# Weight sums of a Strassen-type product: which of them are made by adding transfers and which by VectorE

## The chip, the cores and the metric

The kernel runs on one core of a Trainium2 chip. The metric is device time in microseconds (us), the median of several executions. The engines named here are PE (TensorE, matrix products), DVE (VectorE), ACT (ScalarE), POOL (GpSimd) and SP (SyncE). SP and POOL issue most of the DMA transfers, each into a queue of its own. A DMA issued by POOL can add what it carries to what lies at its destination; such a DMA is called an adding transfer here.

## The reference

One block of a streaming encoder on 256 frames of width 2048, all in float32: a half-step SwiGLU FFN, then two token mixers side by side (banded attention over chunks and retention) merged by sigmoid gates, then a second half-step FFN, and a final norm.

```python
def swiglu_ffn(x, w_gate, w_up, w_down):
    return (jax.nn.silu(x @ w_gate) * (x @ w_up)) @ w_down

x = x + 0.5 * swiglu_ffn(rmsnorm(x, norm_ffn1_g), ffn1_w_gate, ffn1_w_up, ffn1_w_down)
proj = rmsnorm(x, norm_mix_g) @ w_in                      # nine parts, 11264 columns
...                                                       # attention and retention
merged = sigmoid(gate_a) * (att @ w_out_att) + sigmoid(gate_r) * (ret @ w_out_ret)
x = x + merged @ w_out
x = x + 0.5 * swiglu_ffn(rmsnorm(x, norm_ffn2_g), ffn2_w_gate, ffn2_w_up, ffn2_w_down)
return rmsnorm(x, norm_final_g)
```

D_FF is 5632. Nearly all the time is matrix products of 256 rows with weights that are read once from DRAM.

## The kernel before

**Products.** A weight chunk has 2 x 128 rows and 512 columns (a tile 128 x 1024 in float32, 512 KB). Each product is made of three: the weight is split into a rounded part `hi` (an ACT copy, line 140) and the rest `lo` (a DVE subtraction, line 141), and `three` (lines 151, 152, 154) multiplies activation-hi by `hi`, activation-lo by `hi`, and last activation-hi by `lo`. So PE waits for `lo` only at line 154, after four or more products with `hi`.

**Steps.** The work of PE is a list of steps, one per weight chunk. A standard step (class `Gemm`: the down products, some projections) makes 12 products, a step of the class `Strassen` makes 6. `run` goes through the list. Ahead of a step it calls `prep_upto`, which writes the split of the steps up to four ahead into the streams of ACT and DVE (there are four split buffers), and then the work that `later(n, ...)` has put off by n steps.

**Groups.** A `Strassen` object computes two blocks of 512 columns at once, here w1 and w2 (for an FFN: up and gate), with seven products of half size in place of eight. With `a0`, `a1` for the upper and lower rows of w1 and `b0`, `b1` for those of w2, each of the four chunks jc = 0..3 passes through these sums:

- `loads`: tile `k` gets a0 and tile `x` gets b0, by DMAs on POOL's queue (line 540).
- first sum: x = b0 + a0. Either DVE makes it (`first`, line 529) or an adding transfer from tile to tile on POOL's queue (`add_on`, line 545).
- second sum: x = x + b1 (line 597, DVE). b1 is in the tile `raw` that SP's queue fetched for a product of its own.
- `third`: k = x - a0 on DVE (line 583), and then x = x + a1 by an adding transfer from DRAM (line 584).

A group has seven runs of four steps, named by phase and kind: phase 0 has `r` (a0) and `s` (the first sum), phase 1 `r` (b1) and `s` (the second sum), phase 2 `r` (a1) and `s` (k), phase 3 `s` (x after the third). The tile names say it: `loz15401s` is the `lo` part of group z154, phase 0, jc 1, kind s; a name `lo<-raw,hi` without a z belongs to a standard step. `weave` puts standard steps between the steps of the groups.

There are 26 groups: ten in each FFN (the names z10 to z334 and z706 to z1030) and six in the mixer's projections (z390 to z565). `ADDED`, `MIX_ADDED` and `FIRST_ADDED` say for which jc the first sum is an adding transfer: none in the first group of the mixer and of the second FFN; jc 2 and 3 in the very first group, z10; jc 0 in the mixer's other five and in the second group of each FFN (z46, z742); jc 0 and 1 in the other sixteen groups of the FFNs.

**Order.** Engines work through their streams in order. POOL's stream is nearly only DMA issues. SP fetches `raw` tiles into five buffers, as soon as one is free.

Of the kernel before, what the change touches and what calls it, by code (L numbers as in the profile page):

```python
# [11 lines left out]
ALU = mybir.AluOpType  # L12
# [29 lines left out]
RET_WAIT = (14, 6)  # L42
RET_PUT = ((3, 5), (2, 2))
HELD = 6
MIX_ADDED = (0,)
FIRST_ADDED = (2, 3)
MIX_AHEAD = 12
FIRST_WAIT = 4
LAST_SUM = 24
ROTATED = {("q", 0): (6, 7), ("k", 0): (5, 6), ("q", 1): (4, 5), ("k", 1): (3, 4)}  # L50
HEAD_AT = (3, 6, 10, 13, 17, 20, 24, 27)

MIX_SHARE = (0.5,) * 4 + (1.0,) * 4 + (0.0,) * 4 + (0.2,) * 4
SHARE = (0.75,) * 4 + (1.0,) * 4 + (0.0,) * 4 + (0.2,) * 4
ADDED = (0, 1)
ADD_WAIT = 6
PLAIN = 10
PASSES = ((10,),) + tuple((b,) for b in range(10))
# [28 lines left out]
def block_kernel(ctx: ExitStack, tc: tile.TileContext, x, g1, w1g, w1u, w1d, gm, w_in, rel, woa, wor, wo,  # L87
                 g2, w2g, w2u, w2d, gf, cos, sin, decay, ident, out):
    nc = tc.nc
# [30 lines left out]
    def later(n, fn):  # L120
        due.setdefault(state["step"] + n, []).append(fn)

    def weights_tile(name):
        return wpool.tile([P, KC, NB], F32, tag="raw", bufs=RAW_BUFS, name=name)

    def chunk(w, r0, c0):
        return w[r0 : r0 + KC * P, c0 : c0 + NB].rearrange("(k p) n -> p k n", p=P)

    def fetch(t, w, r0, c0, parts=(slice(0, KC),)):
        for p in parts:  # L130
            nc.sync.dma_start(t[:, p, :], chunk(w, r0, c0)[:, p, :])

    def split_tiles(name):
        return [
            wpool.tile([P, KC, NB], F32R, tag=tag, bufs=SPLIT_BUFS, name=f"{tag}{name}") for tag in ("hi", "lo")
        ]

    def split(raw, name):
        hi, lo = split_tiles(name)
        nc.scalar.copy(hi, raw)  # L140
        nc.vector.tensor_sub(lo, raw, hi.bitcast(F32))  # L141
        return hi, lo
# [3 lines left out]
    def three(products, read_between=False):  # L146


        more = {"skip_group_check": True} if read_between else {}
        for acc, (ahi, alo), (whi, _), first, _ in products:  # L150
            nc.tensor.matmul(acc, ahi, whi, start=first, stop=False, **more)  # L151
            nc.tensor.matmul(acc, alo, whi, start=False, stop=False, **more)  # L152
        for acc, (ahi, _), (_, wlo), _, last in products:
            nc.tensor.matmul(acc, ahi, wlo, start=False, stop=last, **more)  # L154
# [216 lines left out]
    class Operand:  # L371


        def __init__(self, name, n):
            self.hi, self.lo, self.name = [None] * n, [None] * n, name
# [18 lines left out]
    class Norm:  # L394
# [40 lines left out]
        def put(self, b, halves=(0, 1), between=None):  # L435
# [28 lines left out]
            elif 1 in halves and b % 2 == 1:  # L464
                for i, key in enumerate(self.SUMS):
                    wait = LAST_SUM if key == "s7" and self.name != "n1" and b == D // NB - 1 else 1 + 3 * i
                    later(wait, lambda key=key: self.add_up(b // 2, key))
# [39 lines left out]
    class Strassen:  # L507
# [3 lines left out]

        def __init__(self, norm, w1, col1, w2, col2, evict, added=()):
            self.added, self.summed = added, set()
            self.add_wait, self.early = ADD_WAIT, False
            self.norm, self.w, self.col, self.evict = norm, (w1, w2), (col1, col2), evict
            self.x, self.kept, self.acc, self.wide = {}, {}, {}, {}
            self.name = f"z{len(steps)}"
# [17 lines left out]
        def loads(self):  # L535
# [11 lines left out]
            def second(jc):  # L547
# [3 lines left out]
                elif self.early:  # L551
                    later(FIRST_WAIT, lambda: self.first_once(jc))

# [16 lines left out]
        def step(self, phase, jc, of_sum):  # L570
            made = {}
            name = f"{self.name}{phase}{jc}{'rs'[of_sum]}"
            n = HALF_K // KC

            def load():
                made["raw"] = weights_tile(f"raw{name}")
                i = 2 - phase
                fetch(made["raw"], self.w[i], self.rows(1, jc), self.col[i])

            def third():  # L580

                x, k = self.x[jc], self.kept[jc]
                nc.vector.tensor_sub(k, x, k)
                nc.gpsimd.dma_start(x, chunk(self.w[0], self.rows(1, jc), self.col[0]), accum_op=ALU.add)

            def prep():
                x = self.x[jc]
                if not of_sum:
                    if phase == 0:
                        made["w"] = split(self.kept[jc], name)  # L590
                        if jc not in self.added and not self.early:
                            self.first_once(jc)
                        return
                    raw = made.pop("raw")
                    made["w"] = split(raw, name)
                    if phase == 1:
                        nc.vector.tensor_add(x, x, raw)
                elif phase == 2:
                    made["w"] = split(self.kept.pop(jc), name)
                elif phase == 3:  # L600
                    made["w"] = split(self.x.pop(jc), name)
                else:
                    if phase == 0:
                        self.first_once(jc)
                    made["w"] = split(x, name)
                    if phase == 1:
                        third()

            bank, form, fresh, closing = {
# [4 lines left out]
            }[phase, of_sum]  # L614

            def products():
                hi, lo = made["w"]
                if fresh and jc == 0:
                    self.bank(bank)
                three([  # L620
                    (
                        self.acc[bank], self.norm.form(form, KC * jc + i), (hi[:, i, :], lo[:, i, :]),
                        fresh and jc == 0 and i == 0, closing and jc == n - 1 and i == KC - 1,
                    )
                    for i in range(KC)
                ], True)
                if jc == n - 1:
                    self.end(phase, of_sum)

            loaded = not of_sum and phase in (1, 2)  # L630
            frees = ["raw"] if loaded else ["kept"] if of_sum and phase > 1 else []
            return Step(self, 0, load if loaded else None, prep, frees, products)

        def end(self, phase, of_sum):
# [103 lines left out]
    def ffn(name, norm, wg, wu, wd, after, start=None):  # L738
# [41 lines left out]
        def paired(b):  # L780
# [10 lines left out]

            return Strassen(norm, wu, b * NB, wg, b * NB, evict, ADDED)

# [282 lines left out]
    def gates(col1, col2, func, dsts):  # L1076
# [9 lines left out]

        return Strassen(nm, w_in0, col1, w_in0, col2, evict, MIX_ADDED)

# [6 lines left out]
    def queries():  # L1095
# [9 lines left out]

        return Strassen(nm, w_in0, QA, w_in0, QA + NB, evict, MIX_ADDED)

# [90 lines left out]
    def at(step, fn):  # L1198
        due.setdefault(step, []).append(fn)
# [60 lines left out]
    for step, fn in merges:  # L1260
        at(step - 8, fn)
# [64 lines left out]
```

## Time and profile before

| | before |
|---|---|
| median of 3 runs | 2037.09 us (2036.96 to 2037.99) |
| profiled execution | 2037.64 us |
| its span, first to last instruction | 2035.9 us |
| PE busy | 2023.9 us (99%) |
| DVE busy | 1786.5 us (88%) |
| ACT busy | 1504.3 us (74%) |
| POOL busy | 342.9 us (17%) |
| moved by DMA | 504.77 MB |
| of it on POOL's queue (q0) | 196.80 MB |
| of it on SP's queue (q1) | 297.31 MB |
| granted clock of PE | 0.999 |

The time of an execution is some 2 us more than its span. A row of the timeline has the start and the length of an instruction in us, engine, line, operation and tiles, its form, and in square brackets how long the engine had stood idle and who ended that. Instructions on DVE overlap a little: one that follows on another starts before the other's recorded end. A row of windows ends with the granted clock, the share of time in which the 16 DMA engines were at work (records overlap, so it can pass 1), and GB/s.

### The profile page before, as it was taken

The page shows a single profiled execution, that of the slowest core. Times are in us where ns is not written, and L with a number is a line of the kernel's source. Part 1 is how long each engine was busy: PE and PEld are TensorE (multiplying, and loading weights), DVE is VectorE, ACT ScalarE, POOL GpSimd, SP SyncE. Part 2 cuts the span into 40 slices and gives each one's busy share as a digit, 9 for nine tenths or more (in the row PEclk, how much of TensorE's full clock was granted, in tenths as well). Part 3 has the DMA queues.
Part 4 walks back from the last instruction along what each step waited for, and adds up shares of the span by engine and source line. Part 5 has one row for each costly group of instructions (what it writes and reads, how often), then busy time and mean ns, then how long its engine had stood idle before and what let it go on. Part 6 is the DMA issues. An engine that isn't in the chain of part 4 may idle for free.

```text
span 2035.9 us, 26220 instructions
## 1 busy us (share of the span) xinstructions
PE 2023.9 (99%) x9170; PEld 1678.8 (82%) x9170; DVE 1786.5 (88%) x1823; ACT 1504.3 (74%) x1886; POOL 342.9 (17%) x399
## 2 busy tenths in 40 slices
PE   9999999999999999999999999999999999999998
PEld 7788888888888888888888888888888888888886
DVE  7999999999998898999987677569999999999996
ACT  7788888878888777777765434557788888888885
POOL 1221122212112021111120000011112221122200
PEclk9999999999999999999999999999999999999999
DMA  9888899988878689899897645576889988889974
GB/s 311 255 249 258 255 269 281 262 240 250 260 235 237 218 232 303 273 283 286 256 320 236 209 156 185 186 247 188 263 268 276 274 243 237 258 269 270 285 199 135
DMA packets 226436, 504.77 MB, mean 248 GB/s; under 512 B 15776, under 2 KB 16480, under 8 KB 226304
## 3 DMA queue, kind: packets, MB, share of 16 engines
q1 hardware_dynamic: 154560, 297.31, 43.1%
q0 software_dynamic: 67536, 196.80, 37.4%
q10 hardware_dynamic: 4208, 8.99, 1.2%
q8 instruction: 72, 1.18, 0.2%
q14 instruction: 60, 0.49, 0.1%
HBM read 471.04 MB, written 10.50 MB: 237 GB/s over the span
## 4 chain that ended last, share of the span: by engine, by line
PE 98%; DVE 0%; DMA 0%; ACT 0%; issue 0%; POOL 0%; DVEq 0%; POOLq 0%; ACTq 0%; SPq 0%
PE acc L152 15%; PE acc L151 15%; PE acc L154 15%; DMA raw<-in_ffn_w_gate_dram 0%; PE z298a L152 0%; PE z530a L151 0%; PE z425a L151 0%; PE z850a L152 0%; PE z154a L152 0%; PE z1030a L152 0%; PE z994a L152 0%; PE z565a L151 0%; PE z742a L152 0%; PE z334a L152 0%; PE z118a L152 0%; PE z886a L152 0%
## 5 line engine op out<-in xcount | busy, mean ns | idle before, releaser
L141 DVE TENSOR_TENSOR lo<-raw,hi 128x1024 fp32r<-128x1024 f32 x351 | 427.7, 1221 | 118.7 <-ACT hi L140 113.8
L140 ACT CAST hi<-raw 128x1024 fp32r<-128x1024 f32 x351 | 368.0, 1050 | 178.0 <-PE acc L152 134.0
L808 ACT ACTIVATE xall<-acc 128x512 f32<-128x512 f32 x160 | 94.6, 591 | 13.4 <-PE acc L154 9.3
L805 ACT ACTIVATE acc<-xall 128x512 f32<-128x512 f32 x160 | 95.9, 600 | 2.5
L151 PE MATMUL acc<-hi,mgh 128*128 128x512 f32 x128 | 50.2, 392 | 0.0
L152 PE MATMUL acc<-hi,mgl 128*128 128x512 f32 x128 | 49.8, 389 | 0.0
L154 PE MATMUL acc<-lo,mgh 128*128 128x512 f32 x128 | 35.5, 390 | 0.0
L151 PE MATMUL acc<-hi,nma01h 128*128 128x512 f32 x80 | 32.0, 400 | 0.0
L151 PE MATMUL acc<-hi,nma00h 128*128 128x512 f32 x80 | 31.9, 398 | 0.0
L152 PE MATMUL acc<-hi,nma01l 128*128 128x512 f32 x80 | 31.2, 390 | 0.0
L152 PE MATMUL acc<-hi,nma00l 128*128 128x512 f32 x80 | 31.2, 390 | 0.0
L151 PE MATMUL acc<-hi,nma11h 128*128 128x512 f32 x80 | 31.2, 390 | 0.0
L151 PE MATMUL acc<-hi,nma10h 128*128 128x512 f32 x80 | 31.2, 390 | 0.0
L152 PE MATMUL acc<-hi,nma11l 128*128 128x512 f32 x80 | 31.2, 390 | 0.0
L152 PE MATMUL acc<-hi,nma10l 128*128 128x512 f32 x80 | 31.2, 390 | 0.0
L154 PEld LDWEIGHTS acc<-lo,mgh 128*128 128x128 f32 x128 | 24.0, 188 | 5.0
L151 PEld LDWEIGHTS acc<-hi,mgh 128*128 128x128 f32 x128 | 24.0, 188 | 4.9
L152 PEld LDWEIGHTS acc<-hi,mgl 128*128 128x128 f32 x128 | 24.1, 188 | 4.8
L151 PE MATMUL acc<-hi,atth 128*128 128x512 f32 x64 | 25.7, 402 | 0.0
L151 PE MATMUL acc<-hi,reth 128*128 128x512 f32 x64 | 25.3, 395 | 0.0
L359 POOL TENSOR_TENSOR n2rstd<-v,mhalf 128x2 f32<-128x2 f32 x1 | 0.7, 695 | 144.6 <-DVE v L358 144.6
L152 PE MATMUL acc<-hi,attl 128*128 128x512 f32 x64 | 25.0, 390 | 0.0
(6885 smaller groups left out, 7279.9 us busy)
## 6 DMA issues: line engine op xcount, KB each, us to landing
raw<-in_ffn_w_down_dram SPq DMA_DIRECT2D x176, 512.0 KB, 7.1
raw<-in_w_in_dram SPq DMA_DIRECT2D x80, 512.0 KB, 5.7
raw<-in_w_out_dram SPq DMA_DIRECT2D x32, 512.0 KB, 3.7
raw<-in_ffn_w_up_dram SPq DMA_DIRECT2D x16, 512.0 KB, 4.9
raw<-in_w_out_att_dram SPq DMA_DIRECT2D x16, 512.0 KB, 3.9
raw<-in_w_out_ret_dram SPq DMA_DIRECT2D x16, 512.0 KB, 3.7
raw<-in_ffn_w_gate_dram SPq DMA_DIRECT2D x15, 512.0 KB, 4.9
z390x<-in_w_in_dram POOLq DMA_DIRECT2D x8, 512.0 KB, 8.8
```

The source lines that it names most:

```text
L140: nc.scalar.copy(hi, raw)
L141: nc.vector.tensor_sub(lo, raw, hi.bitcast(F32))
L151: nc.tensor.matmul(acc, ahi, whi, start=first, stop=False, **more)
L152: nc.tensor.matmul(acc, alo, whi, start=False, stop=False, **more)
L154: nc.tensor.matmul(acc, ahi, wlo, start=False, stop=last, **more)
L359: nc.gpsimd.tensor_tensor(dst, v, mhalf[:, :width], op=ALU.pow)
L805: nc.scalar.activation(acc, xs[t][:, cols], AF.Copy, scale=2.0)
L808: nc.scalar.activation(xs[t][:, cols], acc, AF.Copy, scale=0.5)
```

## The change

The first sums are now all made by DVE but for the two of z10 (jc 2 and 3). The second sums are no longer made by DVE: an adding transfer reads b1 from DRAM again and adds it to `x`. It is put off by two steps behind the split of the step phase 0 `s` of the same jc. The tile `raw` with b1 is still fetched by SP for its own product.

```diff
-MIX_ADDED = (0,)
+MIX_ADDED = ()
 FIRST_ADDED = (2, 3)
...
+SECOND_WAIT = 2
...
-ADDED = (0, 1)
+ADDED = ()
...
-            self.add_wait, self.early = ADD_WAIT, False
+            self.add_wait, self.early, self.adds_second = ADD_WAIT, False, True
...
+            def second():
+                nc.gpsimd.dma_start(self.x[jc], chunk(self.w[1], self.rows(1, jc), self.col[1]), accum_op=ALU.add)
...
                     made["w"] = split(raw, name)
-                    if phase == 1:
+                    if phase == 1 and not self.adds_second:
                         nc.vector.tensor_add(x, x, raw)
...
                     if phase == 0:
                         self.first_once(jc)
                     made["w"] = split(x, name)
+                    if phase == 0 and self.adds_second:
+                        later(SECOND_WAIT, second)
                     if phase == 1:
                         third()
```

The streams of PE, ACT and SP keep their order. In the streams of DVE and POOL rows appear and go. Below, a number behind a tile's name is its buffer, and lines 141, 529, 540, 545, 583 and 584 of before are lines 142, 530, 541, 546, 587 and 588 of the changed kernel.

DVE at the beginning of phase 0 of group z154, one of the sixteen groups, before:

```order
L141 TENSOR_TENSOR loz15400r<-z154k_2035,hiz15400r 128x1024
L141 TENSOR_TENSOR loz15401r<-z154k_2443,hiz15401r 128x1024
L141 TENSOR_TENSOR lo_2618<-raw_2417,hi_2617 128x1024
L141 TENSOR_TENSOR loz15400s<-z154x_2059,hiz15400s 128x1024
L788 SCALAR_TENSOR_TENSOR z118c_2557<-z118a,n1rstd,z118c_2557 128x512
L141 TENSOR_TENSOR loz15402r<-z154k_2499,hiz15402r 128x1024
L529 TENSOR_TENSOR z154x_2511<-z154x_2511,z154k_2499 128x1024
```

and the same place now:

```order
L142 TENSOR_TENSOR loz15400r<-z154k_2033,hiz15400r 128x1024
L530 TENSOR_TENSOR z154x_2057<-z154x_2057,z154k_2033 128x1024
L142 TENSOR_TENSOR loz15401r<-z154k_2442,hiz15401r 128x1024
L530 TENSOR_TENSOR z154x_2473<-z154x_2473,z154k_2442 128x1024
L142 TENSOR_TENSOR lo_2618<-raw_2416,hi_2617 128x1024
L142 TENSOR_TENSOR loz15400s<-z154x_2057,hiz15400s 128x1024
L794 SCALAR_TENSOR_TENSOR z118c_2555<-z118a,n1rstd,z118c_2555 128x512
L142 TENSOR_TENSOR loz15402r<-z154k_2498,hiz15402r 128x1024
L530 TENSOR_TENSOR z154x_2510<-z154x_2510,z154k_2498 128x1024
```

The first sums of jc 0 and 1 now stand in front of the `lo` of the standard step (`lo_2618`).

DVE at the beginning of phase 1 of the same group, before:

```order
L141 TENSOR_TENSOR loz15410r<-rawz15410r,hiz15410r 128x1024
L597 TENSOR_TENSOR z154x_2059<-z154x_2059,rawz15410r 128x1024
L141 TENSOR_TENSOR loz15411r<-rawz15411r,hiz15411r 128x1024
L597 TENSOR_TENSOR z154x_2474<-z154x_2474,rawz15411r 128x1024
L141 TENSOR_TENSOR lo_2784<-raw_2621,hi_2783 128x1024
L141 TENSOR_TENSOR loz15410s<-z154x_2059,hiz15410s 128x1024
```

and now:

```order
L142 TENSOR_TENSOR loz15410r<-rawz15410r,hiz15410r 128x1024
L142 TENSOR_TENSOR loz15411r<-rawz15411r,hiz15411r 128x1024
L142 TENSOR_TENSOR lo_2785<-raw_2621,hi_2784 128x1024
L142 TENSOR_TENSOR loz15410s<-z154x_2057,hiz15410s 128x1024
L587 TENSOR_TENSOR z154k_2033<-z154x_2057,z154k_2033 128x1024
```

The second sums are gone from DVE; what follows them has moved up.

POOL from the last loads of z154 to the third sums, before:

```order
L540 DMA z154x_2547<-in_ffn_w_gate_dram 128x2x512
L545 DMA z154x_2474<-z154k_2443 128x1024
L540 DMA z190k_2563<-in_ffn_w_up_dram 128x2x512
L540 DMA z190x_2587<-in_ffn_w_gate_dram 128x2x512
L545 DMA z190x_2587<-z190k_2563 128x1024
L584 DMA z154x_2059<-in_ffn_w_up_dram 128x2x512
```

and now:

```order
L541 DMA z154x_2546<-in_ffn_w_gate_dram 128x2x512
L541 DMA z190k_2561<-in_ffn_w_up_dram 128x2x512
L541 DMA z190x_2585<-in_ffn_w_gate_dram 128x2x512
L582 DMA z154x_2057<-in_ffn_w_gate_dram 128x2x512
L582 DMA z154x_2473<-in_ffn_w_gate_dram 128x2x512
L582 DMA z154x_2510<-in_ffn_w_gate_dram 128x2x512
L582 DMA z154x_2546<-in_ffn_w_gate_dram 128x2x512
L588 DMA z154x_2057<-in_ffn_w_up_dram 128x2x512
```

The two adding transfers from tile to tile are gone, and four from DRAM (line 582) stand between the next group's first loads and the third sums.

## Prediction

> **What bounds the kernel now.** I first read the page's busy times, then windows, then the timeline of one group.
>
> ```profile
> PE 2023.9 (99%) x9170; PEld 1678.8 (82%) x9170; DVE 1786.5 (88%) x1823; ACT 1504.3 (74%) x1886; POOL 342.9 (17%) x399
> 500.00:550.00 50.00, 50.00 (x227) 41.48 (x226) 45.70 (x44) 41.61 (x52) 10.13 (x12) 1.00 0.89 263
> 0.00:50.00 50.00, 47.30 (x208) 37.34 (x209) 36.66 (x46) 38.53 (x69) 9.31 (x17) 1.00 0.94 317
> 50.00:100.00 50.00, 49.49 (x220) 39.91 (x219) 49.97 (x53) 39.47 (x48) 14.25 (x16) 1.00 0.87 246
> 2000.00:2050.00 50.00, 27.13 (x131) 22.74 (x130) 21.28 (x32) 17.19 (x33) 1.12 (x2) 0.92 0.22 73
> ```
>
> In a window the columns are PE, PE's weight loads, DVE, ACT and POOL, then clock, DMA share and GB/s. From about 90 us to the tail PE is busy in every microsecond at full clock. All its idle time is 2035.9 - 2023.9 = 12.0 us: 2.7 us in the first 50 us, 0.5 us in the next 50, and 35.9 - 27.1 = 8.8 us behind 2000 us, in the tail. So VectorE, at 88%, does not set the end, and what the change takes off it is worth nothing by itself. The question is whether anything now makes PE wait.
>
> How near PE is to waiting is read from the gap between the end of a `lo` on DVE and PE's first product with it. Group z154, one of the sixteen FFN groups with two adding transfers before:
>
> ```profile
> 281.41 1.22 DVE L141 TENSOR_TENSOR loz11833s<-z118x,hiz11833s 128x1024 fp32r<-128x1024 f32 x1 [1.87 <-ACT hiz11833s L140]
> 282.55 0.68 DVE L659 TENSOR_TENSOR z118c<-z118c,z118s 128x512 f32<-128x512 f32 x1
> 283.15 1.22 DVE L141 TENSOR_TENSOR loz15400r<-z154k,hiz15400r 128x1024 fp32r<-128x1024 f32 x1
> 284.29 1.22 DVE L141 TENSOR_TENSOR loz15401r<-z154k,hiz15401r 128x1024 fp32r<-128x1024 f32 x1
> 285.42 1.22 DVE L141 TENSOR_TENSOR lo<-raw,hi 128x1024 fp32r<-128x1024 f32 x1
> 286.56 1.22 DVE L141 TENSOR_TENSOR loz15400s<-z154x,hiz15400s 128x1024 fp32r<-128x1024 f32 x1
> 286.87 0.62 PE L154 MATMUL z154a<-loz15401r,n1a00h 128*128 128x512 f32 x2
> 288.23 0.61 PE L154 MATMUL acc<-lo,f1a2h 128*128 128x512 f32 x2
> 290.95 0.62 PE L154 MATMUL z154c<-loz15400s,n1s5h 128*128 128x512 f32 x2
> ```
>
> DVE waits for ACT at 281.41 and then runs without a pause, one 128x1024 operation every 1.135 us. PE takes `loz15401r` 286.87 - 285.51 = 1.36 us after its end, the standard `lo` 288.23 - 286.64 = 1.59 us, `loz15400s` 290.95 - 287.78 = 3.17 us. These are the margins that the change eats.
>
> **The change part by part.** *First sums.* The engine's existing first sums show the price:
>
> ```profile
> L529 DVE TENSOR_TENSOR z154x<-z154x,z154k x2: 1217/1217/1217, 289.5 to 292.9; 128x1024 f32<-128x1024 f32 x2
> L545 POOL DMA_DIRECT2D z82x<-z82k x2: 927/927/927, 111.9 to 155.6; - x2
> L545 POOL DMA_DIRECT2D z1030x<-z1030k x2: 924/927/930, 1875.1 to 1919.7; - x2
> 1502.79 1.22 DVE L141 TENSOR_TENSOR lo<-raw,hi 128x1024 fp32r<-128x1024 f32 x1
> 1505.60 0.61 PE L154 MATMUL acc<-lo,f2a0h 128*128 128x512 f32 x2
> ```
>
> By the stream of the changed kernel, both added sums of such a group stand ahead of the standard `lo`, one of them ahead of `loz15401r`. Beginning at 283.15 as before (DVE still starts on ACT's `hiz11833s`, whose stream is the same), DVE runs `loz15400r` 283.15, sum 284.29, `loz15401r` 285.42, sum 286.56, `lo` 287.69 to 288.91. `loz15401r` keeps 1.36 - 1.14 = 0.22 us. The standard `lo` is late: PE wants it at 288.23. How long after the end of a late `lo` PE goes on is seen in z10, where PE did wait a little:
>
> ```profile
> 78.10 1.22 DVE L141 TENSOR_TENSOR loz1020r<-rawz1020r,hiz1020r 128x1024 fp32r<-128x1024 f32 x1
> 79.37 0.73 PE L154 MATMUL z10b<-loz1020r,n1a01h 128*128 128x512 f32 x2
> ```
>
> The `lo` ends at 79.32, PE starts at 79.37: 0.05 us. So PE starts at 288.96 instead of 288.23: **0.73 us lost**. PE has no idle time later in the group to make it good, and ACT and DVE reach the next group's start paced by PE, so each group loses it anew. Behind it all later margins are shortened by 2 x 1.135 = 2.27 us and lengthened by the 0.73 us that PE is later: `loz15400s` keeps 1.6 us. ACT's `hiz15400s` must now wait for the first sum's end at 285.51, some 0.8 us later than it began, but it was not DVE's limit there.
>
> The pattern is the same in z82 to z334 and in z778 to z1030 (the rows at 1502.79 and 1505.60: 1505.60 - 1504.01 = 1.59 us again, lost 0.73 us): 16 x 0.73 = **+11.7 us**. Bounds: 0 if the chain began earlier than I think; and, if the 0.22 us of `loz15401r` were not there either, 16 x 2.27 = 36 us as the whole of the added DVE time. I take 11.7, since both ends of the subtraction are rows.
>
> In z46 and z742 only one sum joins, and DVE stood idle for 0.90 us where it lands; in the five mixer groups also one, with a nearest margin of 886.89 - 884.87 = 2.02 us against 1.135 us of delay. Both cost nothing; if that slack were gone, 7 x 1.1 = 8 us.
>
> ```profile
> 102.81 1.23 DVE L141 TENSOR_TENSOR lo<-raw,hi 128x1024 fp32r<-128x1024 f32 x1 [0.90 <-ACT hi L140]
> 883.65 1.22 DVE L141 TENSOR_TENSOR loz49500s<-z495x,hiz49500s 128x1024 fp32r<-128x1024 f32 x1
> 886.89 0.62 PE L154 MATMUL z495c<-loz49500s,nms5h 128*128 128x512 f32 x2
> ```
>
> *Second sums off DVE.* 104 of 1.135 us go, 39 come: 65 x 1.135 = 74 us less DVE work, in phase 1, where PE does not wait now. Only z10 gains: PE's 0.5 us of idle time between 50 and 100 us lies behind its phase 1 backlog, as at 79.37. **-0.5 us** (bounds 0 and -0.5).
>
> *Second sums on the DMA.* The nearest rows are the third sums, the same kind and size from DRAM:
>
> ```profile
> L584 POOL DMA_DIRECT2D z154x<-in_ffn_w_up_dram x4: 1194/1194/1211, 309.8 to 323.4; - x4
> DMA to landing us min/median/max: 5.7/6.2/13.3
> 293.88 0.92 POOL L545 DMA_DIRECT2D z190x<-z190k  x1 [13.90 <-DMA z190x<-in_ffn_w_gate_dram]
> 309.83 1.21 POOL L584 DMA_DIRECT2D z154x<-in_ffn_w_up_dram  x1 [15.02 <-ACT xall L808]
> 304.28 1.06 ACT L140 CAST hiz15410s<-z154x 128x1024 fp32r<-128x1024 f32 x1 [0.59 <-PE acc L152]
> 317.34 1.06 ACT L140 CAST hiz15413s<-z154x 128x1024 fp32r<-128x1024 f32 x1 [1.13 <-DVE z154x L597]
> 297.50 1.22 DVE L141 TENSOR_TENSOR loz15403s<-z154x,hiz15403s 128x1024 fp32r<-128x1024 f32 x1
> ```
>
> POOL has nothing else to do between 294.8 and 309.8, so it issues each second sum when the `lo` of its first sum is done: jc 0 near 290 (287.8 + 2.27), jc 3 near 301 (298.7 + 2.27). On POOL only the third sums queue behind these waits, and they come later anyway. Landing after some 6 us means 296 and 307, wanted by ACT at 304.3 and 317.3: 8 to 10 us to spare, and even the longest landing, 13.3 us, reaches jc 3 only at 314. Cost 0.
>
> What remains is the bandwidth.
>
> ```profile
> 254.00:290.00 36.00, 36.00 (x160) 29.84 (x159) 33.27 (x32) 28.39 (x34) 10.40 (x12) 1.00 1.04 318
> 290.00:314.00 24.00, 24.00 (x111) 19.96 (x111) 22.60 (x22) 20.76 (x27) 2.13 (x2) 1.00 0.66 175
> 254.00:314.70 60.70, 60.70 (x273) 50.38 (x272) 56.58 (x53) 49.14 (x60) 12.53 (x14) 1.00 0.89 260
> 854.00:911.00 57.00, 57.00 (x253) 47.20 (x252) 53.96 (x49) 41.76 (x45) 11.49 (x14) 1.00 0.93 287
> q0 software_dynamic: 545, 1.07, 72.2%
> q1 hardware_dynamic: 564, 1.09, 38.1%
> q0 software_dynamic: 544, 1.05, 53.8%
> q0 software_dynamic: 148, 0.54, 20.8%
> ```
>
> The last four rows are queues, with packets, MB and share of the 16 engines. From 862 to 870 us POOL's queue q0 carries third sums: 0.722 x 8 us for 1.07 MB, so 2.8 us of all 16 engines for 0.52 MB; SP's q1 stands below it. From 310 to 322 us it is 0.538 x 12 us for 1.05 MB, 3.2 us for 0.52 MB. From 292 to 309 us q0 has one adding transfer between tiles: 0.208 x 17 = 3.5 us. An FFN group gains 4 x 2.8 and loses 2 x 3.5: +4.2 us on 54 of 60.7, so 0.95 to 0.96, against 1.04 in the stretch where the engines are full. They land where the share is 0.66, between the full stretches. A mixer group gains 11.2 - 3.5 = 7.7 us on 53 of 57: 1.06, just what a full stretch shows. I take 0 for the FFNs and 0 for the mixer, with 10 us as the mixer's upper bound: 60.7 us of load less 1.04 x 57 = 59.3 is 1.4 us per group, and at 3.2 us per second sum 3.0 us. Six groups give 8 to 18 us before buffers take any of it; I put it at 10.
>
> The Trainium skill, "DMA: Bandwidth & Descriptors", section "Anatomy of one DMA", gives the data part of a transfer as bytes over 436 GB/s, 1.2 us for 0.52 MB. The rows above have 2.8 us for an adding one, so here the measurement decides; by the page the mixer group would stay at 0.95 and the sum the same.
>
> **Sum.** In the profiled execution: 2037.64 + 11.7 - 0.5 = 2048.8 us. The median of the runs is 0.55 us under that execution, so I predict **2048.3 us**.
>
> **Rivals.**
> - *Hidden: no measurable change, 2036.6 us* (2037.1 - 0.5). DVE would have to start its chain at least 0.7 us earlier against PE. For it: ACT loses a wait for the old adding transfer at jc 1:
>
> ```profile
> 289.36 1.05 ACT L140 CAST hiz15401s<-z154x 128x1024 fp32r<-128x1024 f32 x1 [2.59 <-DMA z154x<-z154k]
> ```
>
>   Against: that wait of 2.59 us lies behind the late `lo`, and the chain starts on ACT's `hi` for the group before.
> - *DMA full: slower still, about 2058 us.* In the mixer `raw` tiles or the next group's `k` and `x` land late, as the shares allow: 2048.3 + 10. It decides from the point where the mixer's load passes what a full stretch carries. In its favour, 1.06 by shares; against it, shares are swollen by contention, and each mixer group has a stretch of low share. The same skill page, section "Issuing engines are not separate DMA queues", says that transfers from all queues share the 16 engines; the trace agrees (from 862 to 870 us the shares of the two queues sum to 1.10).
> - *Faster, between 2025 and 2033 us.* VectorE at 88% is the hidden bound, and 74 us less work shortens stalls that PE's row does not show, the matmuls being modelled. The most it can give is all of PE's idle time: 2037.1 - 12.0 = 2025 us. But the margins above are positive everywhere outside z10, so 0.5 us is all that I can find.
> - *The second sums are still on DVE*: no, the stream shows them gone.
>
> **How the numbers follow.** Late `lo`: 0.66. DMA full on top of it: 0.17. Hidden: 0.12. Faster: 0.05. Within the likeliest case I expect 2044 to 2053 us (0.45 to 1.0 us lost per group). To hold the time 8 times in 10 the range reaches into the DMA case and towards the hidden one: 2040 to 2061 us. A measurement of this kernel tells about 0.2% (4 us) from no change. Slower by more than that takes the first two cases less a part that comes out under 4 us: 0.80. Within: 0.16. Faster: 0.04.
>
> **What would show it.** In the changed profile: PE idle time of some 0.7 us once in each of the sixteen groups, before a product of line 154 with a standard `lo`, put down to DVE, with two sums ahead of it; groups 61.4 us apart instead of 60.7; no PE idle time in phase 1 and in z46 and z742; DVE busy near 1786 - 65 x 1.2 = 1708 us; second sums landed well before their `hi` on ACT; about 54.5 - 20.4 = 34 MB more moved. It is wrong if PE shows no idle time there, or if it waits for ACT behind `raw`, `k` or `x` landing late, above all between 750 and 1050 us.

## The result and the profile after

| | before | after |
|---|---|---|
| median of 4 runs each, on one chip | 2037.39 us | **2051.14 us** (2050.79 to 2052.51) |
| ratio, with its 95% interval | | 1.0068 (1.0056 to 1.0081) |
| profiled execution | 2037.64 us | 2052.51 us |
| its span | 2035.9 us | 2050.7 us |

The change costs 13.7 us. The changed kernel's page, engines first, then what was moved and POOL's queue (packets, MB, share of the 16 engines):

```profile
PE 2029.5 (99%) x9170; PEld 1677.1 (82%) x9170; DVE 1727.2 (84%) x1758; ACT 1503.2 (73%) x1886; POOL 432.3 (21%) x464
DMA packets 249111, 538.87 MB, mean 263 GB/s; under 512 B 16817, under 2 KB 17521, under 8 KB 248977
q0 software_dynamic: 90208, 230.88, 46.4%
```

DVE has 65 instructions fewer and 59 us less busy time, 34.1 MB more were moved, and the span is 14.8 us longer. PE has as many products as before. Its busy time grew by 5.6 us; the rest is 9.2 us more idle time. Windows of the changed kernel (PE, weight loads, DVE, ACT, POOL, clock, DMA share, GB/s) say where:

```profile
50.00:100.00 50.00, 48.88 (x216) 39.13 (x215) 45.06 (x48) 38.38 (x47) 15.66 (x17) 1.00 1.03 286
500.00:550.00 50.00, 49.45 (x222) 40.69 (x221) 45.82 (x43) 40.09 (x50) 13.02 (x15) 1.00 0.98 287
850.00:900.00 50.00, 50.00 (x222) 41.39 (x221) 44.36 (x40) 34.97 (x38) 13.07 (x14) 1.00 1.06 333
900.00:950.00 50.00, 50.00 (x223) 41.39 (x222) 44.02 (x40) 37.56 (x41) 13.01 (x14) 1.00 1.07 315
```

An FFN window that was full before now has 0.55 us of idle time (500 to 550 us); z10's window has lost another 0.6 us (it had 49.49); the mixer's windows are full, though their DMA share is 1.06 to 1.07.

The beginning of group z154 in the changed kernel's timeline (start, length; the last row of PE has the idle time and its releaser in brackets):

```profile
285.33 1.22 DVE L142 TENSOR_TENSOR loz15400r<-z154k,hiz15400r 128x1024 fp32r<-128x1024 f32 x1
286.46 1.22 DVE L530 TENSOR_TENSOR z154x<-z154x,z154k 128x1024 f32<-128x1024 f32 x1
287.60 1.22 DVE L142 TENSOR_TENSOR loz15401r<-z154k,hiz15401r 128x1024 fp32r<-128x1024 f32 x1
288.73 1.22 DVE L530 TENSOR_TENSOR z154x<-z154x,z154k 128x1024 f32<-128x1024 f32 x1
289.87 1.22 DVE L142 TENSOR_TENSOR lo<-raw,hi 128x1024 fp32r<-128x1024 f32 x1
289.05 0.63 PE L155 MATMUL z154a<-loz15401r,n1a00h 128*128 128x512 f32 x2
291.14 0.73 PE L155 MATMUL acc<-lo,f1a2h 128*128 128x512 f32 x2 [0.55 <-DVE lo L142]
291.71 0.39 PE L152 MATMUL acc<-hi,f1a2h 128*128 128x512 f32 x1
```

The standard `lo` ends at 291.09 behind two sums, and PE starts its product 0.05 us later, after a wait that the profile puts at 0.55 us. (That is less than the delay: the product ahead of it has a recorded length that runs past its successor's usual start.) One group earlier the same row stands at 229.51 us, so the groups are 61.63 us apart instead of 60.73. Over the program the view of waits has

```profile
PE acc L155 <- DVE lo L142: 8.9, 16, 0.6
ACT hi L141 <- DMA raw<-in_ffn_w_down_dram: 39.4, 34, 2.5
```

The first row (total, times, longest) is PE waiting for a standard `lo`: sixteen times, 0.56 us in the mean. No such row stands among the waits before. The second row was 2.9 us in 3 waits before: ACT now waits for `raw` tiles that land later, nearly always hidden.

PE's products, matched one to one between the two profiled executions, put its delay together: -0.49 us by the first product of z10 (the startup of the two executions), +0.83 in z10, +0.03 in z46, +7.19 in the eight groups z82 to z334, 0.00 from z390 through the mixer to z706, -0.34 in z706, +7.84 in z778 to z1030: 15.07 us. The FFN groups lose 0.87 to 0.91 us each; in z958 and z994 some more is added.

### The profile page after: what moved, and what is told of

It reads as the page before. It is cut to its first block, busy times and chain, and to the rows that moved or that the text cites. A ratio compares the mean times of both kernels' runs of the same rounds, so it can differ in the third digit from the quotient of the medians.

```text
span 2050.7 us, 26355 instructions
## 1 busy us (share of the span) xinstructions
PE 2029.5 (99%) x9170; PEld 1677.1 (82%) x9170; DVE 1727.2 (84%) x1758; ACT 1503.2 (73%) x1886; POOL 432.3 (21%) x464
## 4 chain that ended last, share of the span: by engine, by line
PE 92%; DVE 3%; issue 2%; DMA 1%; ACT 0%; POOL 0%; DVEq 0%; POOLq 0%; ACTq 0%
PE acc L155 15%; PE acc L152 15%; PE acc L153 15%; DVE lo L142 1%; DMA z10x<-in_ffn_w_gate_dram 1%; DMA z10x<-z10k 0%; PE z425a L153 0%; PE z425a L152 0%; PE z530a L152 0%; PE z495a L152 0%; PE z460a L152 0%; PE z565a L152 0%; PE z390a L153 0%; PE z425a L155 0%; PE z706a L153 0%
## 5 line engine op out<-in xcount | busy, mean ns | idle before, releaser
L141 ACT CAST hi<-raw 128x1024 fp32r<-128x1024 f32 x351 | 368.0, 1050 | 238.2 <-PE acc L153 138.6
```

## Experiments

The **late-`lo` theory**: in an FFN group, PE loses what DVE puts ahead of a standard `lo` beyond the margin that this `lo` had, plus the price of starting again. The rivals put the loss to the traffic of the second sums, or to the amount of work on DVE. All kernels below are the changed kernel with the edit shown; times stand against runs of the kernel before on the same chip (2037.3 to 2037.4 us). "Loss per group" is how much later the next group's first product on PE comes, against the kernel before, than this group's own first product, in the profiled executions. Behind the last group, z1030, it is counted to PE's last product.

### The two halves of the change alone

First sums only (the second sums stay on DVE):

```diff
-            self.add_wait, self.early, self.adds_second = ADD_WAIT, False, True
+            self.add_wait, self.early, self.adds_second = ADD_WAIT, False, False
```

> Only the first sums move to DVE; the second sums stay on DVE, so there are 41 adding transfers fewer than before and 104 fewer than in the changed kernel, and DVE has all the sums but two. Late-lo theory: the whole loss is there, 16 x 0.9 = 14 us over before, 2050 to 2053 us, with the wait of 0.55 us in front of the standard lo's product in the sixteen groups. If phase 1 margins (0.44 to 1.15 us before, with 2.27 us more DVE work ahead of them less PE's 0.9 us of lateness) are also used up, more: up to 2065 us. DMA theory: no loss, about 2037 us.

Measured: 2051.05 us, ratio 1.0067 (1.0052 to 1.0082). The page of that kernel, and z154 in its timeline:

```profile
PE 2029.2 (99%) x9170; PEld 1678.1 (82%) x9170; DVE 1830.0 (89%) x1862; ACT 1504.0 (73%) x1886; POOL 307.1 (15%) x360
```

```profile
288.92 1.22 DVE L142 TENSOR_TENSOR lo<-raw,hi 128x1024 fp32r<-128x1024 f32 x1
290.19 0.73 PE L155 MATMUL acc<-lo,f1a2h 128*128 128x512 f32 x2 [0.53 <-DVE lo L142]
```

The whole loss is there without one second sum on the DMA: 0.90 us per group in the first FFN, 0.87 in the second, and nothing in z10 and the mixer. The DMA theory of the loss has fallen. The amount of DVE work is no cause either: 1830 us here, 1727 in the changed kernel, the same time.

Second sums only (the first sums stay adding transfers):

```diff
-MIX_ADDED = ()
+MIX_ADDED = (0,)
...
-ADDED = ()
+ADDED = (0, 1)
```

> Only the second sums move to adding transfers; the first sums stay as in the kernel before (adding transfers for jc 0 and 1 in the sixteen groups). 145 adding transfers in place of the changed kernel's 104, DVE busy about 1680 us. Late-lo theory: no sum is put ahead of the standard lo, so no PE wait there; 2037 to 2039 us (the 1.2 us of z10 at 55 us stays), groups of the FFN 60.7 us apart. DMA theory (the extra transfers make loads land late and PE wait): as slow as the changed kernel or slower, 2051 to 2060 us.

Measured: **2072.54 us**, ratio 1.0174 (1.0159 to 1.0190). This was not expected: without a sum ahead of any `lo`, the loss is 35 us, 21 us more than the whole change. Rows of its timeline:

```profile
237.00 0.94 POOL L546 DMA_DIRECT2D z154x<-z154k  x1 [14.16 <-DMA z154x<-in_ffn_w_gate_dram]
237.59 2.81 POOL L582 DMA_DIRECT2D z118x<-in_ffn_w_gate_dram  x2
262.85 1.04 ACT L141 CAST hi<-raw 128x1024 fp32r<-128x1024 f32 x1 [3.05 <-DMA raw<-in_ffn_w_down_dram]
263.94 0.80 PE L152 MATMUL acc<-hi,f1a1h 128*128 128x512 f32 x1 [1.90 <-ACT hi L141]
```

Windows, columns as above:

```profile
500.00:550.00 50.00, 49.94 (x221) 40.15 (x220) 41.33 (x38) 38.03 (x47) 11.60 (x13) 1.00 1.07 315
850.00:900.00 50.00, 48.98 (x214) 39.44 (x213) 41.74 (x38) 33.46 (x37) 15.25 (x17) 1.00 1.05 286
```

The view of line 582, the second sums, from issue to landing:

```profile
DMA to landing us min/median/max: 5.8/11.9/18.2
```

PE now waits for `hi`, ACT for a `raw` that lands late: the sign of the "DMA full" rival, in a kernel that is not the changed one. An FFN window has a share of 1.07, where the changed kernel has 0.98. The second sums take 11.9 us to land in the median; in the changed kernel it is 6.1 us. There are two candidate causes: too many bytes and adding transfers (an FFN group has two transfers between tiles more than the changed kernel), or the order on POOL. There the first sum of the next group, z154, waits 14 us for its tile, and the second sums of z118 stand behind it: issued at 237.6 and not near 229 and 233.

### One, one and a half, two, three operations ahead

One sum ahead: jc 1's first sum goes back to an adding transfer.

```diff
-ADDED = ()
+ADDED = (1,)
```

> As the changed kernel, but jc 1's first sum is an adding transfer between tiles again wherever there is a second group member before it; only jc 0's sum (1.135 us) stands ahead of the standard lo. Late-lo theory, with a margin of 1.59 us as threshold: 1.135 is under it, so no PE wait, 2037 to 2040 us. Rival (each sum ahead costs its share, no threshold): half of the loss, about 2044 us. DMA theory: second sums and added transfers together, 2051 us or more.

One and a half: the same, with half an operation more on DVE behind the split of phase 0 `r` jc 1, in the sixteen groups.

```diff
-ADDED = ()
+ADDED = (1,)
...
+                        if jc == 1 and self.many:
+                            nc.vector.tensor_tensor(self.kept[0][:, 0, :], self.kept[0][:, 0, :], self.kept[0][:, 0, :], op=ALU.max)
...
+            group.many = n > 1 and extra > 0 and ahead == 8
```

> The kernel with jc 1's first sum as an adding transfer (one sum ahead, no loss) with half an operation more on DVE ahead of the standard lo in the sixteen groups (the maximum of half of tile k of jc 0 with itself, 128x512, about 0.6 us; the result is the same). Late-lo theory with a threshold of 1.59 us: 1.135 + 0.6 - 1.59 + 0.05 = 0.2 us of wait and 0.15 us for going on, 16 x 0.35 = 5.6 us over that kernel, 2042 to 2046 us. Rival (a loss in proportion to the work ahead, 0.9 us for 2.27): 16 x 0.9 x 0.6 / 1.135 = 7.6 us more than with one sum, and already there with one sum, which the run with one sum has not shown. Rival (no loss below two whole sums): 2038 us.

Three: the changed kernel with a whole such operation at that place.

```diff
+                        if jc == 1 and self.many:
+                            nc.vector.tensor_tensor(self.kept[0], self.kept[0], self.kept[0], op=ALU.max)
```

> The changed kernel with one more 128x1024 operation on DVE (the maximum of tile k of jc 0 with itself, the result is the same) ahead of the standard lo in each of the sixteen groups: 3 x 1.135 = 3.41 us ahead instead of 2.27. Late-lo theory, with every us above the margin of 1.59 us lost in full: 16 x 1.135 = 18 us over the changed kernel, 2067 to 2072 us. In the run with the seconds only, PE ran at a granted clock of 0.60 for some 4 us behind an idle time of 1.9 us; if that comes here too, with 1.9 us of idle time per group, up to 16 x 1.5 us more, to 2095 us. Rival (the loss is something fixed per group, such as the restart of PE, and does not grow with the work ahead): no change from the changed kernel, 2051 us.

With the margin of 1.59 us, 0.05 us to go on, and 0.11 us for going on (below):

| ahead of the standard `lo` | kernel | worked out | loss per group | median |
|---|---|---|---|---|
| 1.135 us | one | none | 0.00 to 0.09 | 2038.32 (ratio 1.0005, 0.9995 to 1.0014) |
| 1.135 + 0.61 | one and a half | 0.205 + 0.11 = 0.32 | 0.33 to 0.41 | 2043.63 (1.0030, 1.0018 to 1.0041) |
| 2.27 | changed | 0.73 + 0.11 = 0.84 | 0.87 to 0.91 | 2051.14 (1.0068) |
| 3.41 | three | 1.87 + 0.11 = 1.98 | 2.00 to 2.05 | 2071.13 (1.0164, 1.0149 to 1.0179) |

(Left out are z958 and z994 of the changed kernel, and z1030, behind which the tail is counted in: 2.29 us with three, 0.10 with one.) Rows of z154 with one and a half, and with three; in both the product starts 0.05 us behind the end of `lo`:

```profile
288.53 0.68 DVE L596 TENSOR_TENSOR z154k<-z154k 128x512 f32<-128x512 f32 x1
289.14 1.22 DVE L142 TENSOR_TENSOR lo<-raw,hi 128x1024 fp32r<-128x1024 f32 x1
290.41 0.73 PE L155 MATMUL acc<-lo,f1a2h 128*128 128x512 f32 x2
```

```profile
294.45 1.23 DVE L142 TENSOR_TENSOR lo<-raw,hi 128x1024 fp32r<-128x1024 f32 x1
295.73 0.74 PE L155 MATMUL acc<-lo,f1a2h 128*128 128x512 f32 x2 [1.67 <-DVE lo L142]
```

Below the margin next to nothing is lost (0.09 us at most), and above it every microsecond is lost in full. The kernel with one sum ahead has all 104 second sums and 18 transfers between tiles more than the changed kernel (DVE 1707.9 us, 548.31 MB moved), and its time is that of the kernel before within what can be measured.

### The same work in another order

jc 1's first sum behind the first standard `lo` instead of ahead of it:

```diff
-                        if jc not in self.added and not self.early:
+                        if jc not in self.added and not self.early and jc != 1:
                             self.first_once(jc)
...
+                    if phase == 0 and jc == 0 and not self.early:
+                        self.first_once(1)
```

> The same instructions on DVE and the same transfers as the changed kernel, but jc 1's first sum stands behind the standard lo instead of ahead of it. Late-lo theory: only one sum is ahead, no PE wait in the sixteen groups, 2037 to 2040 us (z10's 1.2 us stays). Rivals that go by the amount of work on DVE or by the traffic: no change from the changed kernel, 2050 to 2052 us.

Measured: 2047.75 us, ratio 1.0051 (1.0034 to 1.0068). Neither side: the wait at the first `lo` is gone, but half of the sixteen groups still lose 0.41 to 0.46 us in the profiled execution, and the others 0.7 to 1.8 us, where ACT also waits for a late `raw` (that execution was 2.8 us above the median). The kernel before and this one at the second standard `lo` of z154, 9 us on:

```profile
294.03 1.22 DVE L141 TENSOR_TENSOR lo<-raw,hi 128x1024 fp32r<-128x1024 f32 x1
297.29 0.62 PE L154 MATMUL acc<-lo,f1a2h 128*128 128x512 f32 x2
```

```profile
296.98 1.23 DVE L142 TENSOR_TENSOR lo<-raw,hi 128x1024 fp32r<-128x1024 f32 x1
298.25 0.74 PE L155 MATMUL acc<-lo,f1a2h 128*128 128x512 f32 x2
```

Before, this `lo` had a margin of 297.29 - 295.25 = 2.04 us. Both sums, 2.27 us, are ahead of it wherever the second stands: 2.27 - 2.04 + 0.05 + 0.11 = 0.39 us, and 0.41 to 0.46 were measured. In these eight groups the theory holds; the expectation had applied it to one `lo` only. In the other eight, what the late `raw` adds is not worked out. In the changed kernel this second wait does not show, because PE has already been made 0.84 us later.

So both places were relieved: jc 3's first sum goes behind the second `lo` too.

```diff
-                        if jc not in self.added and not self.early:
+                        if jc not in self.added and not self.early and jc not in (1, 3):
                             self.first_once(jc)
...
+                    if phase == 0 and jc == 0 and not self.early:
+                        self.first_once(1)
+                    if phase == 0 and jc == 2 and not self.early:
+                        self.first_once(3)
```

> All the DVE work and all the transfers of the changed kernel, but jc 1's first sum stands behind the first standard lo of the group and jc 3's behind the second (the one that is ready 8 to 9 us later and was found late by 0.23 us with jc 1's sum moved alone: margin 2.04 us in the kernel before against 2.27 us of sums ahead). Late-lo theory: 1.135 us ahead of the first (margin 1.59), 2.27 - 1.135 = 1.135 us ahead of the second (margin 2.04): no wait for either, 2037 to 2041 us. Rival (the DVE work or the traffic as such costs): 2047 us or more, as with jc 1's sum moved alone.

Measured: **2086.87 us**, ratio 1.0243 (1.0228 to 1.0258), a loss of 2.74 to 2.79 us in nearly every one of the sixteen groups. The expectation failed altogether. ACT and PE in z154:

```profile
305.74 1.05 ACT L141 CAST hiz15403s<-z154x 128x1024 fp32r<-128x1024 f32 x1 [4.93 <-DVE z154x L530]
310.31 1.04 ACT L141 CAST hiz15410r<-rawz15410r 128x1024 fp32r<-128x1024 f32 x1
306.84 0.50 PE L152 MATMUL z154c<-hiz15403s,n1s5h 128*128 128x512 f32 x1 [0.38 <-ACT hiz15403s L141]
312.93 0.50 PE L152 MATMUL z154c<-hiz15410r,n1s3h 128*128 128x512 f32 x1 [1.12 <-ACT z154s L652]
```

The first reader of a sum is not the product but ACT's `hi`, and ACT works in order. It stood still for 4.93 us in front of `hiz15403s`, and the splits behind it came late too: PE waits here, a little at the `lo` of the same tile, and 1.12 us for phase 1's first `hi`. The view of waits has no row of PE waiting for a standard `lo` any more: the late `lo` is gone, but the price went to the engine whose queue had not been looked at.

### Why the second sums alone cost 35 us

jc 0's transfer between tiles is put off by eight steps, so that it stands behind the second sums on POOL:

```diff
-MIX_ADDED = ()
+MIX_ADDED = (0,)
...
-ADDED = ()
+ADDED = (0, 1)
...
-                    later(self.add_wait, lambda: add_on(jc))
+                    later(self.add_wait + (8 if jc == 0 else 0), lambda: add_on(jc))
```

> The seconds-only kernel (first sums as before on adding transfers), which took 2072 us, with jc 0's adding transfer between tiles put off by eight steps more, behind the four second sums of the group ahead of it on POOL's queue instead of in front of them. The same number of transfers and bytes. Queue theory (the loss comes from second sums that queue on POOL behind an adding transfer that waits for its tile to land): most of the 35 us goes, 2038 to 2045 us. DMA theory (the engines are full: the sum of the shares is about 1.08 of the group's time): the loss stays, 2065 to 2075 us.

Measured: 2092.34 us, ratio 1.0270 (1.0253 to 1.0287). The edit went too far in the groups that had little time to spare:

```profile
94.90 0.91 POOL L546 DMA_DIRECT2D z46x<-z46k  x1 [1.05 <-DMA z46k<-in_ffn_w_up_dram]
112.32 1.04 ACT L141 CAST hiz4600s<-z46x 128x1024 fp32r<-128x1024 f32 x1 [9.02 <-DMA z46x<-z46k]
113.42 0.80 PE L152 MATMUL z46c<-hiz4600s,n1s5h 128*128 128x512 f32 x1 [4.89 <-ACT hiz4600s L141]
```

z46 lost 8.9 us, z425 13.5 and z742 7.4, where the first sum itself comes late. As a whole it decides nothing. In z82 to z334 and z778 to z1030, where the put-off sum had time, the loss is 7.0 us and 9.0 us, against 15.4 us and 11.9 us with the seconds only. So in the FFNs the order is a part of it.

The cleaner pair: jc 0's sum as the adding transfer and jc 1's on DVE, against the kernel with jc 1's as the adding transfer. The transfers, the bytes and the sums ahead of `lo` are the same in number.

```diff
-ADDED = ()
+ADDED = (0,)
```

> As the kernel with jc 1's first sum as an adding transfer, but it is jc 0's that is the adding transfer, and jc 1's is made by DVE. The number of transfers, the bytes and the sums ahead of the standard lo (one) are the same as there; the difference is that jc 0's adding transfer stands on POOL in front of the group before's second sums, as in the seconds-only kernel. Load theory for the 35 us of the seconds-only kernel (two transfers between tiles per group are too many beside four second sums, one is not): 2037 to 2041 us. Queue theory (the second sums come late because jc 0's transfer is in front of them on POOL): at least half of the 2.2 us per group that the seconds-only kernel lost in the sixteen groups, 2053 us or more.

Measured: 2044.05 us, ratio 1.0033 (1.0020 to 1.0046), where its twin took 2038.32. POOL's timeline, and the landing of the second sums in the view of line 582:

```profile
231.30 0.93 POOL L546 DMA_DIRECT2D z154x<-z154k  x1 [16.58 <-DMA z154x<-in_ffn_w_gate_dram]
231.89 1.57 POOL L582 DMA_DIRECT2D z118x<-in_ffn_w_gate_dram  x1
```

```profile
DMA to landing us min/median/max: 5.7/8.2/17.1
```

The twin's row reads 5.8/6.3/11.9. With equal load, the exchange costs 5.7 us between the medians (six runs from 2040.53 to 2045.89 us; the profiled execution, at 2041.25 us, is one of the faster ones) and makes the second sums land later. That is less than the queue theory asked for and a little more than the load theory allowed. The other 28 us of the 2072.54 appear only with the second transfer between tiles per FFN group and the one per mixer group. That most of this is load is argued, not shown, because the second transfer also stands on POOL's queue. In the profiled executions the sixteen groups lose 0.8 us with jc 1's transfer alone and 2.9 us with jc 0's alone; with both they lose 16.0 us with jc 0's put off and 27.2 us with the seconds only. So the second transfer costs much in either order, and with two of them the order is worth 11 us more. How much is bytes, how much the adding itself and how much the waits at the head of POOL's queue was not separated.

### z10's second sums back on DVE

```diff
             if n == 0 and start is not None:
                 group.add_wait = 2
+                group.adds_second = False
```

> The changed kernel with the second sums of the very first group, z10, back on DVE; all else as changed. The question is the wait of 1.2 us at 55 us, where hiz1003s waits 3.37 us for z10x. Queue theory (the adding transfer of jc 3's first sum stands on POOL behind jc 0's second sum, which waits for DVE): that wait goes, PE busy 49.4 to 49.5 us between 50 and 100 us as before instead of 48.88. Rival (the first sums' adding transfers are slowed by the number of bytes under way, not by the order on POOL): PE still loses about 1 us there. The sixteen groups lose 0.9 us each as in the changed kernel; the whole about 1 us under it, 2049 to 2051 us.

One run: 2050.59 us; the reading is in the trace. In the changed kernel, POOL and ACT in z10's timeline, and the view of line 546, the adding transfers from tile to tile:

```profile
43.32 1.23 POOL L582 DMA_DIRECT2D z10x<-in_ffn_w_gate_dram  x1 [3.74 <-DVE loz1000s L142]
44.05 1.44 POOL L546 DMA_DIRECT2D z10x<-z10k  x1
54.24 1.05 ACT L141 CAST hiz1003s<-z10x 128x1024 fp32r<-128x1024 f32 x1 [3.37 <-DMA z10x<-z10k]
```

```profile
DMA to landing us min/median/max: 7.2/8.7/10.1
```

and with z10's second sums on DVE, the same two views and the window:

```profile
42.28 0.88 POOL L546 DMA_DIRECT2D z10x<-z10k  x1 [3.16 <-DMA z10x<-in_ffn_w_gate_dram]
50.48 1.04 ACT L141 CAST hiz1003s<-z10x 128x1024 fp32r<-128x1024 f32 x1
```

```profile
DMA to landing us min/median/max: 6.7/7.0/7.3
```

```profile
50.00:100.00 50.00, 49.50 (x219) 39.91 (x218) 49.97 (x53) 39.44 (x48) 13.34 (x15) 1.00 0.88 260
```

ACT's wait of 3.37 us is gone and the window is back at 49.50 us: the wait belongs to z10's second sums. All nine profiled kernels that have them on the DMA show it (1.1 to 3.4 us), and none of the three that have them on DVE. The expectation wanted to tell the order on POOL from the bytes under way. The edit takes both away, so it can't. Two things differ in the rows: jc 3's first sum is issued 1.8 us earlier here (1.5 with the startup taken out), and it takes 6.7 instead of 10.1 us. The 10.1 us is the longest of the nine; in the other eight it lands after 7.9 to 9.4 us.

## Why the prediction was right, point by point

The forecast was 2048.3 us by a late `lo` in the sixteen groups; 2051.14 us were measured, and the late `lo` it is.

- *What bounds the kernel.* Right: 59 us of busy time taken off DVE gained 0.8 us (z10 and z706), and with the first sums only, at 1830 us of it, the loss was the same.
- *First sums, "0.73 us lost".* The step is right, and the delay up to the start of that product is as worked out. The term was **mis-sized**: a group loses 0.89 us, so that 16 groups cost 14.2 us and not 11.7. After the wait, the product pair takes 291.71 - 291.14 = 0.57 us to the next product, where it took 0.45 without one; that is 0.11 us which the prediction left out. The remaining 0.05 us is a lateness that FFN 1 also shows with one sum ahead (up to 0.09 us at one product with `hi`) and FFN 2 hardly; its cause is open.
- *"`loz15401r` keeps 0.22 us", "`loz15400s` keeps 1.6 us".* The first ends at 288.82 and is used at 289.05, so 0.23 us. No wait at either. The second standard `lo`, with a margin of 2.04 us, was not looked at; it would have been late by itself, and PE's earlier delay hid it.
- *z46, z742 and the mixer cost nothing.* Right: 0.03, 0.00 and 0.00 us.
- *"Only z10 gains": -0.5 us.* **Wrong in sign** in the profiled execution. A gain of 0.47 us came, and z706 gained 0.34 that had not been seen. But that the size fits is luck. PE's 0.5 us of idle time, from which the term was read, is one wait in phase 2, and it stayed:

```profile
88.22 0.73 PE L154 MATMUL z10b<-loz1023r,n1a01h 128*128 128x512 f32 x2 [0.51 <-DVE loz1023r L141]
```

```profile
88.54 0.73 PE L155 MATMUL z10b<-loz1023r,n1a01h 128*128 128x512 f32 x2 [0.48 <-DVE loz1023r L142]
```

  The gain came in four steps of some 0.12 us between 73 and 81 us, at products with `lo` that were a little late before and at which the profile counts no idle time. And z10 lost 1.3 us at 55 us, 0.83 in all. The step that failed is "on POOL only the third sums queue behind these waits": in z10, jc 3's first sum is an adding transfer on the same queue, behind jc 0's second sum. The size of this loss is that of one execution: in the nine profiled kernels with z10's second sums on the DMA, z10's balance runs from -0.51 to +1.73 us, against +0.01 and +0.03 in the two edited kernels that have them on DVE.
- *Second sums on the DMA, cost 0.* Right for the FFNs and, against its bound of 10 us, for the mixer: PE's delay does not change by 0.01 us over six groups, with shares of 1.01 to 1.07 in the 50-us windows from 750 to 1050 us. The shares were well worked out (0.95 to 0.96 expected for an FFN group; 0.92 to 1.03 in 50-us windows). But the spare room is small: two transfers between tiles more per group, and the kernel loses 35 us. In z958 and z994 the changed kernel itself loses 0.3 and 0.5 us beyond the other groups, where ACT waits for a late `raw` (in z994 for 3.54 us up to 1905.70, as a `raw` issued at 1896.74 lands; this is the row of z958):

```profile
1850.17 1.05 ACT L141 CAST hi<-raw 128x1024 fp32r<-128x1024 f32 x1 [2.27 <-DMA raw<-in_ffn_w_down_dram]
```

- *What would show it.* Idle time in all sixteen groups ahead of line 155 (0.56 us as the profile counts it), 34.1 MB more, groups 61.6 us apart (61.4 said), no wait in phase 1. DVE is busy for 1727 us, not 1708. The 65 operations are gone, 65 x 1.135 = 73.8 us, but an operation with a pause behind it counts with its recorded 1.22 us, where one in a chain adds 1.135. The number of pauses between DVE's operations in the trace rose from 321 to 486: 165 x 0.085 = 14.0 us, and 73.8 - 14.0 = 59.8 us, where 59.3 were measured.
- *Rivals.* "Hidden" fell: DVE's chain started no earlier against PE. "DMA full" fell for the changed kernel; late `raw` tiles, its sign, are what PE lost by when the second sums moved without the first ones, though whether bandwidth or POOL's queue made them late is open. "Faster" fell.

The sum of what was missed: +2.5 (sixteen groups), +1.3 (z10), -0.3 (z706), +0.8 (late `raw`) and -0.5 (startup) on the 11.2 us of the prediction gives 15.0, PE's 15.07 us of delay in the profiled execution; the median of the runs lies 1.4 us below that execution.

None of the kernels beats the one before. Of PE's 12 us of idle time there, all but 0.5 us lie in startup and tail, which none of these edits touches.

## What to carry to other kernels

When work is put ahead of an operand on an in-order engine, list the margin of every later operand until that engine next pauses. Here, what exceeded the smallest margin was lost in full and what stayed under it was nearly free, whether the engine's busy time fell (1727 us) or rose (1830 us). Before moving the work further back, look for its first reader: it can be an engine that itself works in order, and here the loss then grew from 0.9 to 2.8 us per group. When sums are moved to a DMA queue, count the transfers between tiles that share it and what waits at the head of the queue.

## What the runs showed of the hardware

- A matmul pair that starts right behind a wait takes 0.57 us to the next product instead of 0.45.
- The granted clock fell after one idle time of 1.90 us, and not after sixteen of 1.66 to 1.71 us. (With jc 0's sums put off by eight steps it fell after 4.89 and 6.36 us too, to 0.50, and after 3.16 us, to 0.76 over the next 3 us.) With the seconds only, behind the wait that ended at 263.94:

```profile
263.90:266.90 3.00, 2.96 (x7) 2.39 (x8) 2.98 (x3) 3.00 (x4) 0.00 (x0) 0.50 1.10 328
266.90:269.00 2.10, 2.10 (x10) 1.67 (x10) 2.10 (x3) 1.96 (x5) 1.05 (x1) 0.93 1.09 253
```

  and with three operations ahead, behind the wait of 1.67 us that ended at 295.73:

```profile
295.50:299.50 4.00, 3.77 (x19) 3.14 (x20) 4.00 (x5) 1.96 (x3) 1.23 (x1) 1.00 0.52 143
```

  Half the clock for some 3.3 us adds about 1.6 us to a wait of 1.9, as an estimate from these windows. The Trainium skill, "TensorE: Matmul & The Clock Gate", section "HAM oscillation — how this bites in real kernels", gives the rule that PE should have no idle gaps above about 3.4 us. Here 1.90 us was enough once (another idle time, of 0.27 us, had ended 0.73 us before it), so the measurement decides: a gap well under that figure can already cost the clock.
